# A hybrid decoder block on one core: another order of scores, products and transposes within a slot

## The chip, the core and the metric

One Trainium2 chip, of which the kernel uses one core. The metric is device microseconds of one execution of the whole program; the median of several executions is compared.

## The reference

One layer of a decoder block for 512 positions and width 1024, in fp32. A combined projection gives q, k and v of 16 heads of width 64: eight with dilated sliding-window attention, eight with block-sparse attention. At this length both are causal softmax attention with a bias per head:

```python
u = rmsnorm(h, g_mix[l])
qa, ka, va, qb, kb, vb = jnp.split(u @ w_in[l], 6, axis=-1)
ya = dilated_attention(...)
yb = moba_attention(...)
y = jnp.concatenate([rmsnorm(merge(ya, DIL_WIDTH), g_out_dil[l]),
                     rmsnorm(merge(yb, MOBA_WIDTH), g_out_moba[l])], axis=-1)
h = h + y @ w_out[l]
h = h + memory_cross_attention(rmsnorm(h, g_cross[l]), rmsnorm(mem, g_mem[l]), ...)
h = h + conv_ffn(rmsnorm(h, g_ffn[l]), ...)
```

The output is the RMSNorm of h.

## The kernel before

Every large product is made of three fp32r matmuls with high and low parts (hi by hi, hi by lo, lo by hi). Weights come by DMA on SyncE's queue into three `stage` buffers; ScalarE makes the high part (`hi`, L88), VectorE or GpSimd the low part (`lo`, L97). In the slots GpSimd makes it.

The self-attention runs in 18 **slots** (L800 on), one head further in each. Slot s holds the scores **S** of head s (`s_steps`), the transposes **T** of head s-1 (`t_steps`) and the products with V, **O**, of head s-2 (`o_steps`). Each is a generator: S yields three times (the 512-wide row block, the 384-wide one, and the 128- and 256-wide ones together), T three times (`pt0`, `pt1`, `pt2`), O four times (one 512-wide step from `pt0`, one 384-wide from `pt1`, two 256-wide from `pt2`). The string ORDER has ten positions and says whose turn it is at each. Ahead of each position `fill` puts in other TensorE work up to a due number from the table PACE: steps of the q and k projections of later heads (three 512-wide matmuls a step, L268 to L270), of V's second half (L565 to L567), and of the memory's keys and values. A projection may be blocked until enough heads have their scores, and then positions follow each other with no filler between.

What follows a TensorE step goes through `Later`, a list of stages that are issued a given number of steps later; `L.need` issues them at once if a reader comes first. The chains of this case:

- S: VectorE adds the bias strip and takes the maximum (L701), ScalarE the exponential (L706), VectorE the reciprocal (L711); the normalisation (L713) is VectorE's for the two wide row blocks and GpSimd's for the two narrow ones. The result is `P`, of which there are two buffers.
- T: ScalarE copies the high part out of PSUM (`pt0h` and so on, L251), one step later; VectorE subtracts for the low part (`pt0l`, L256), three steps after that.
- O: ScalarE copies half of the product's bank (`tmp`, L251), then VectorE adds (`y`, L778). For every second head ScalarE makes `Y` and its squares, and GpSimd adds the squares to `ssy` (L283), which the norm matmul L301 reads after the slots.
- q and k: VectorE scales (L259), ScalarE copies, VectorE and GpSimd subtract (L532, L548). For k, two DMAs on SyncE's queue (L535, L536) then copy one half to the other partitions.
- `xm` and `mr` (L466, L256) belong to the memory's preparation, which is spread over the slots.

Each engine works through its own instructions in the order in which they were issued. PSUM has two banks `acc` for projections and a ring of six for all `s`, `t` and `o` tiles, given out in the order in which the steps first come. A slot takes seven of them: three S, three T, one O. The strip of biases for head s+2 is loaded on SyncE's queue when head s begins its scores (`load_strip`, L348).

Of the kernel before, what the change touches and what calls it, by code (L numbers as in the profile page):

```python
# [28 lines left out]
C_MIX, C_OUT, C_CROSS, C_MEM, C_FFN, C_FIN, C_CW, C_CB = 0, 8, 16, 24, 32, 40, 48, 48 + 3 * FT  # L29
NVEC = C_CB + FT  # L30
WARM = 9
ORDER = "OOSOOTSTST"
PACE = ((0, 8), (1, 17), (1.8, 24), (5.0, 64), (5.85, 72), (9.1, 112), (11.8, 136), (18, 209))
RM = 13
XL = {0: (4, 5), 1: (6, 7)}
# [137 lines left out]
def block_kernel(tc, xT, x_tok, memT, mem_tok, w_in, w_out, w_q, w_km, w_vm, w_o, w_gu, w_dn, vecs, relT, onehot,  # L173
                 addend, out):
    nc = tc.nc
    with ExitStack() as ctx:
# [108 lines left out]
        def norm_stages(R, ssq, n, d, exact=False):  # L285


            v = {}

            def s0():  # L290
                v["h"] = tmp(F32R)[:, :n]
                copy(v["h"], ssq)

            def s1():
                v["l"] = tmp(F32R)[:, :n]
                sub(v["l"], ssq, bf(v["h"]))

            def s2():
                v["p"] = ps = bank("t")[:, :n]
                if exact:  # L300
                    nc.tensor.matmul(ps, ones32, ssq, start=True, stop=True)  # L301
                else:
                    nc.tensor.matmul(ps, ones, v["h"], start=True, stop=False)
                    nc.tensor.matmul(ps, ones, v["l"], start=False, stop=True)

            def s3():
                v["r"], v["a"] = tmp()[:, :n], tmp()[:, :n]
                nc.scalar.activation(v["r"], v["p"], AF.Abs_reciprocal_sqrt, scale=1.0 / d, bias=epsb)
                nc.scalar.activation(v["a"], v["r"], AF.Square)

            def s4():
                a = v["a"]
                nc.vector.scalar_tensor_tensor(a, v["p"], d * EPS, a, op0=OP.add, op1=OP.mult)
                nc.vector.tensor_scalar(a, a, -0.5 / d, 1.5, op0=OP.mult, op1=OP.add)
                mul(R, a, v["r"])

            return (s2, s3, s4) if exact else (s0, s1, s2, s3, s4)
# [329 lines left out]
        def fill(x):  # L647

            due = np.interp(x, [a for a, _ in PACE], [b for _, b in PACE])
            while filled[0] < due:  # L650
                r = next(fill_gen, "end")
                if r is BLOCK or r == "end":
                    break
                filled[0] += 1
# [140 lines left out]
        def slot_gens(s):  # L795
            return (o_steps(s - 2) if 0 <= s - 2 < 16 else iter(()),
                    t_steps(s - 1) if 0 <= s - 1 < 16 else iter(()),
                    s_steps(s) if s < 16 else iter(()))

        W.lo_eng = tuple(engs[c] for c in LOE)  # L800
        for s in range(18):
            gens = dict(zip("OTS", slot_gens(s)))
            for i, c in enumerate(ORDER):
                fill(s + i / len(ORDER))
                next(gens[c], None)
            for g in gens.values():
                assert next(g, "end") == "end"
            if s == 16:
                ra_tok = L.chain(*norm_stages(SSQ[0], SSQ[0], S, 512), gap=5)
# [482 lines left out]
```

## Time and profile before

| | us |
|---|---|
| median of 3 executions | 784.73 (784.63 to 784.87) |
| the profiled execution | 784.45 |
| its span on the core | 782.7 |
| TensorE busy | 769.5 |
| VectorE, ScalarE, GpSimd busy | 471.3, 384.3, 180.3 |

The span runs from the first to the last instruction; 1.75 us of the profiled execution lie outside it. A matmul's row in the timeline lasts longer than the distance to the next one, because matmuls overlap; what a matmul costs is read from start to start. The slots lie between about 48 and 247 us of the span.

### The profile page before, as it was taken

What the parts mean: (1) busy time and instruction counts of PE and PEld (TensorE: products, weight loads), DVE (VectorE), ACT (ScalarE), POOL (GpSimd) and SP (SyncE); (2) the same over time, 40 slices, a digit from 0 to 9 for tenths busy, and PEclk for the clock granted to TensorE, in tenths of its full rate; (3) what the DMA queues carried; (4) which work ended last, traced back from release to release, by engine and by line L of the source; (5) the groups of instructions that cost most, each with busy time, mean ns of one, the idle gap of its engine ahead of it and who ended that gap; (6) DMA issues with size and microseconds to landing.
All of it is one profiled execution on the core that took longest, in us unless ns stands there. A gap on an engine that the chain in (4) does not pass through costs nothing.

```text
span 782.7 us, 10336 instructions
## 1 busy us (share of the span) xinstructions
PE 769.5 (98%) x3820; PEld 648.9 (83%) x3820; DVE 471.3 (60%) x874; ACT 384.3 (49%) x753; POOL 180.3 (23%) x179
## 2 busy tenths in 40 slices
PE   9999999999999999999999999999999999999995
PEld 7888989779988888888888888888888888888885
DVE  5656686787663885766486666656666564333324
ACT  5866676677777443544446344343443433322322
POOL 1056566566878550000030000000000000000000
PEclk9999999999999999999999999999999999999998
DMA  9544334334444621211232332232222323333303
GB/s 343 207 141 140 110 123 121 124 92 130 134 155 136 224 99 54 81 55 41 94 108 81 113 103 97 92 108 85 103 94 96 107 78 102 97 96 101 100 21 108
DMA packets 28722, 87.94 MB, mean 112 GB/s; under 512 B 3408, under 2 KB 5584, under 8 KB 28288
## 3 DMA queue, kind: packets, MB, share of 16 engines
q1 hardware_dynamic: 26880, 85.73, 34.0%
q10 hardware_dynamic: 1664, 1.38, 0.5%
q8 instruction: 30, 0.49, 0.3%
q14 instruction: 20, 0.16, 0.1%
q0 software_dynamic: 128, 0.17, 0.1%
HBM read 80.93 MB, written 2.14 MB: 106 GB/s over the span
## 4 chain that ended last, share of the span: by engine, by line
PE 88%; DVE 6%; ACT 4%; DMA 1%; issue 1%; SPq 0%; DVEq 0%; POOL 0%; ACTq 0%; POOLq 0%
PE acc L268 17%; PE acc L270 17%; PE acc L269 17%; PE s L270 6%; PE s L269 6%; PE s L268 6%; PE s L431 2%; PE o L757 2%; PE t L728 1%; DVE P L713 1%; ACT P L706 1%; DVE P L701 1%; PE s L696 1%; PE s L695 1%; DMA mr<-in_memT_dram 1%
## 5 line engine op out<-in xcount | busy, mean ns | idle before, releaser
L88 ACT ACTIVATE hi<-stage 128x512 fp32r<-128x512 f32 (+1 forms) x264 | 152.0, 617 | 182.0 <-PE acc L269 130.2
L97 DVE TENSOR_TENSOR lo<-stage,hi 128x512 fp32r<-128x512 f32 (+1 forms) x178 | 120.2, 711 | 63.0 <-ACT hi L88 63.0
L268 PE MATMUL acc<-X,hi 128*128 128x512 f32 x352 | 140.3, 399 | 0.0
L270 PE MATMUL acc<-X,lo 128*128 128x512 f32 x352 | 137.4, 390 | 0.0
L97 POOL TENSOR_TENSOR lo<-stage,hi 128x512 fp32r<-128x512 f32 x86 | 112.5, 1331 | 29.6 <-ACT hi L88 28.5
L269 PE MATMUL acc<-X,hi 128*128 128x512 f32 x304 | 118.6, 390 | 0.0
L270 PEld LDWEIGHTS acc<-X,lo 128*128 128x128 f32 x352 | 66.0, 188 | 14.2
L268 PEld LDWEIGHTS acc<-X,hi 128*128 128x128 f32 x352 | 66.2, 188 | 11.4 <-issue 0.2
L268 PE MATMUL s<-X,hi 128*128 128x512 f32 x192 | 75.1, 391 | 0.0
L270 PE MATMUL s<-X,lo 128*128 128x512 f32 x192 | 74.7, 389 | 0.0
L268 PE MATMUL acc<-G,hi 128*128 128x512 f32 (+1 forms) x198 | 72.9, 368 | 0.0
L270 PE MATMUL acc<-G,lo 128*128 128x512 f32 (+1 forms) x198 | 72.3, 365 | 0.0
L269 PE MATMUL acc<-G,hi 128*128 128x512 f32 (+1 forms) x198 | 72.3, 365 | 0.0
L269 PE MATMUL s<-X,hi 128*128 128x512 f32 x176 | 68.5, 389 | 0.0
L269 PEld LDWEIGHTS acc<-X,hi 128*128 128x128 f32 x304 | 57.2, 188 | 9.8 <-issue 0.2
L706 ACT ACTIVATE P<-P,st 128x512 f32<-128x512 f32 (+1 forms) x64 | 35.7, 558 | 39.0 <-DVE st L701 38.9
L1084 POOL MEMSET a<- 128x2 f32 x22 | 2.1, 99 | 214.7 <-DVE c L1094 214.0
L1094 DVE SCALAR_TENSOR_TENSOR c<-a,vec,c 128x512 f32<-128x512 f32 x44 | 33.1, 752 | 24.5 <-ACT c L1089 23.8
L268 PEld LDWEIGHTS acc<-G,hi 128*128 128x128 f32 x198 | 37.3, 188 | 6.2
L269 PEld LDWEIGHTS acc<-G,hi 128*128 128x128 f32 x198 | 37.3, 188 | 6.1
L270 PEld LDWEIGHTS s<-X,lo 128*128 128x128 f32 x192 | 36.1, 188 | 7.5
L268 PEld LDWEIGHTS s<-X,hi 128*128 128x128 f32 x192 | 36.0, 188 | 7.6 <-issue 0.2
(264 smaller groups left out, 1536.1 us busy)
## 6 DMA issues: line engine op xcount, KB each, us to landing
stage<-in_w_gu_dram SPq DMA_DIRECT2D x44, 512.0 KB, 3.3
stage<-in_w_in_dram SPq DMA_DIRECT2D x23, 512.0 KB, 3.4
stage<-in_w_dn_dram SPq DMA_DIRECT2D x16, 512.0 KB, 3.5
strip<-scr SPq DMA_DIRECT2D x16, 256.0 KB, 3.9
stage<-in_w_km_dram SPq DMA_DIRECT2D x8, 512.0 KB, 3.5
stage<-in_w_vm_dram SPq DMA_DIRECT2D x8, 512.0 KB, 3.5
stage<-in_w_out_dram SPq DMA_DIRECT2D x8, 512.0 KB, 3.5
stage<-in_w_q_dram SPq DMA_DIRECT2D x8, 512.0 KB, 3.3
```

Source lines behind the costliest of these rows:

```text
L88: self.nc.scalar.activation(self.hi[i][:, a:b], self.stage[i][:, a:b], AF.Copy)
L97: self.lo_eng[part].tensor_sub(self.lo[i][:, a:b], self.stage[i][:, a:b], bf(self.hi[i][:, a:b]))
L268: nc.tensor.matmul(ps, wh[:, w0:w0 + P], xh, start=first, stop=False)
L269: nc.tensor.matmul(ps, wh[:, w0:w0 + P], xl, start=False, stop=False)
L270: nc.tensor.matmul(ps, wl[:, w0:w0 + P], xh, start=False, stop=last)
L431: nc.tensor.matmul(vps[u], (Xl if z == 1 else Xh)[k][:, u * P:(u + 1) * P], w[z // 2][:, ws], start=(k == 0 and z == 0), stop=(k == KT - 1 ...
L695: nc.tensor.matmul(ps[:, o:o + nn], lq, k[:, 0, :nn], start=True, stop=False)
L696: nc.tensor.matmul(ps[:, o:o + nn], lq, k[:, 1, :nn], start=False, stop=True)
L701: nc.vector.tensor_tensor_reduce(v, src, sb[:, :n][:, ::-1], -0.125, 3e38, OP.add, OP.min, accum_out=st[:, i:i + 1])
L706: nc.scalar.activation(v, v, AF.Exp, scale=-1.0, bias=st[:, i:i + 1], accum_out=st[:, 4 + i:5 + i])
L757: nc.tensor.matmul(ps[:, 512 - (b - a):512], V[g][kb][:, j * P:(j + 1) * P], pts[e][pg][z][:, a:b], start=(kb == 0 and z == 0), stop=(kb = ...
L1094: nc.vector.scalar_tensor_tensor(v["c"], v["a"][:, 6 + o:6 + o + S], col(C_CW + o * FT + f), v["c"], op0=OP.mult, op1=OP.add)
```

## The change

ORDER becomes a pair of strings. Slot 0, which has scores alone, keeps the old one. From slot 1 on, scores stand at positions 0, 2 and 8 instead of 2, 6 and 8, products at 1, 3, 4 and 6 instead of 0, 1, 3 and 4, and transposes stay at 5, 7 and 9. The divisor of the position is 10 as before, so the fillers' due numbers are the same.

```diff
-ORDER = "OOSOOTSTST"
+
+ORDER = ("OOSOOTSTST", "SOSOOTOTST")
...
-            for i, c in enumerate(ORDER):
-                fill(s + i / len(ORDER))
+            for i, c in enumerate(ORDER[min(s, 1)]):
+                fill(s + i / 10)
                 next(gens[c], None)
```

Line numbers in the changed file are higher by one below ORDER.

TensorE's order where slot 9 ends and slot 10 begins, before (`t` are transposes, `o` products, `s` scores, `acc` a projection used as filler):

```order
L728 MATMUL t_1772<-ident,P_1562 128x128 x3
L757 MATMUL o_1780<-pt0h_432,V_724 128x512
L757 MATMUL o_1780<-pt0l_433,V_724 128x512
L268 MATMUL acc_1784<-X_110,hi_1592 128x512
L269 MATMUL acc_1784<-X_110,hi_1592 128x512
L270 MATMUL acc_1784<-X_110,lo_1623 128x512
L757 MATMUL o_1780<-pt1h_434,V_724 128x384
L757 MATMUL o_1780<-pt1l_435,V_724 128x384
```

and after:

```order
L729 MATMUL t_1767<-ident,P_1542 128x128 x3
L696 MATMUL s_1782<-K_1685,Q_1592 128x512
L697 MATMUL s_1782<-K_1685,Q_1592 128x512
L269 MATMUL acc_1787<-X_110,hi_1594 128x512
L270 MATMUL acc_1787<-X_110,hi_1594 128x512
L271 MATMUL acc_1787<-X_110,lo_1625 128x512
L758 MATMUL o_1796<-pt0h_432,V_726 128x512
L758 MATMUL o_1796<-pt0l_433,V_726 128x512
L269 MATMUL acc_1787<-X_111,hi_1594 128x512
L270 MATMUL acc_1787<-X_111,hi_1594 128x512
L271 MATMUL acc_1787<-X_111,lo_1625 128x512
L696 MATMUL s_1812<-K_1685,Q_1592 128x384
```

The first score (which reads K5) now stands directly behind the slot's last transpose. The product with `pt0` has five matmuls more between it and that transpose. Behind the rows shown come the second 384-wide score matmul and three more projections, and then the product with `pt1`.

VectorE's order in slot 9, from the first score's normalisation on, before (`ISA` rows are the bias-and-maximum and its read-out):

```order
L713 TENSOR_SCALAR P_1687<-P_1687,st_1688 128x512
L256 TENSOR_TENSOR xm<-mr_1580,xm 128x2x256
L778 TENSOR_TENSOR y_1587<-o_1666,tmp_1714 64x512
L701 ISA P_1687,st_1688<-s_1735,strip_1409 128x384
L701 ISA st_1688 128x1
L256 TENSOR_TENSOR pt0l_433<-t_1723,pt0h_432 128x512
L711 RECIPROCAL st_1688<-st_1688 128x1
L713 TENSOR_SCALAR P_1687<-P_1687,st_1688 128x384
```

and after, from the second score's maximum on:

```order
L702 ISA P_1668,st_1669<-s_1694,strip_1389 128x384
L702 ISA st_1669 128x1
L533 TENSOR_TENSOR K_1685<-tmp_1692,K_1685 64x512
L712 RECIPROCAL st_1669<-st_1669 128x1
L714 TENSOR_SCALAR P_1668<-P_1668,st_1669 128x384
L257 TENSOR_TENSOR xm<-mr_1585,xm 128x2x256
L257 TENSOR_TENSOR pt0l_433<-t_1725,pt0h_432 128x512
L779 TENSOR_TENSOR y_1617<-o_1680,tmp_1739 64x512
L702 ISA P_1668,st_1669<-s_1754,strip_1389 128x128
```

The `y` add moved behind the second score's maximum (`s_1694`) and normalisation and behind `pt0l`; the third score's maximum (`s_1754`) comes behind `y`. The first score's maximum and normalisation stand ahead of these rows in both.

GpSimd's order at the end of the slots, before:

```order
L97 TENSOR_TENSOR lo_2760<-stage_2667,hi_2743 128x512 x2
L283 TENSOR_TENSOR ssy_1965<-ssy_1965,tmp_2773 128x512
L97 TENSOR_TENSOR lo_2789<-stage_2704,hi_2778 128x512 x2
L97 TENSOR_TENSOR lo_2838<-stage_2738,hi_2826 128x512 x2
L97 TENSOR_TENSOR lo_2883<-stage_2767,hi_2868 128x512 x2
```

and after:

```order
L98 TENSOR_TENSOR lo_2756<-stage_2662,hi_2741 128x512 x2
L98 TENSOR_TENSOR lo_2784<-stage_2704,hi_2767 128x512 x2
L284 TENSOR_TENSOR ssy_1999<-ssy_1999,tmp_2787 128x512
L98 TENSOR_TENSOR lo_2838<-stage_2736,hi_2826 128x512 x2
L98 TENSOR_TENSOR lo_2883<-stage_2762,hi_2868 128x512 x2
```

The sum of squares that L301 (L302 after) reads has one more pair of weight operations ahead of it.

## Rows read from the trace of the kernel before

**Rows 1.** The page, part 1: engine, busy us, share, instructions.

```profile
PE 769.5 (98%) x3820; PEld 648.9 (83%) x3820; DVE 471.3 (60%) x874; ACT 384.3 (49%) x753; POOL 180.3 (23%) x179
```

**Rows 2.** TensorE's waits: for whom, us in total, times, longest us.

```profile
PE o L757 <- DVE pt1l L256: 1.1, 4, 0.4
...
PE o L757 <- DVE pt0l L256: 0.5, 1, 0.5
PE o L757 <- ACT pt1h L251: 0.5, 1, 0.5
```

**Rows 3.** TensorE's timeline: start us, us, line, out<-in, [idle before <- releaser].

```profile
64.61 0.33 PE L757 MATMUL o<-pt1h,V 128*128 128x384 f32 x1
64.78 0.34 PE L757 MATMUL o<-pt1l,V 128*128 128x384 f32 x1
...
151.66 0.34 PE L757 MATMUL o<-pt1h,Y 128*128 128x384 f32 x1
152.22 0.44 PE L757 MATMUL o<-pt1l,Y 128*128 128x384 f32 x1 [0.21 <-DVE pt1l L256]
...
153.42 0.39 PE L696 MATMUL s<-K,Q 128*128 128x512 f32 x1
...
155.38 0.28 PE L757 MATMUL o<-pt2l,Y 128*128 128x256 f32 x1
...
160.59 0.49 PE L728 MATMUL t<-ident,P 128*128 128x128 f32 x3
160.83 0.47 PE L757 MATMUL o<-pt0h,V 128*128 128x512 f32 x1
161.76 0.50 PE L757 MATMUL o<-pt0l,V 128*128 128x512 f32 x1 [0.46 <-DVE pt0l L256]
...
162.33 0.39 PE L269 MATMUL acc<-X,hi 128*128 128x512 f32 x1
162.56 0.40 PE L270 MATMUL acc<-X,lo 128*128 128x512 f32 x1
163.41 0.45 PE L757 MATMUL o<-pt1h,V 128*128 128x384 f32 x1 [0.45 <-ACT pt1h L251]
164.24 0.44 PE L757 MATMUL o<-pt1l,V 128*128 128x384 f32 x1 [0.38 <-DVE pt1l L256]
```

**Rows 4.** VectorE's timeline in slot 9 and at the start of slot 10.

```profile
153.94 0.69 DVE L701 CUSTOM_DVE_ANT_0 P<-s,strip 128x512 f32<-128x512 f32 x1 [0.27 <-issue]
...
156.91 0.17 DVE L711 RECIPROCAL st<-st 128x1 f32<-128x1 f32 x1 [1.68 <-ACT P L706]
...
158.01 1.77 DVE L256 TENSOR_TENSOR xm<-mr,xm 128x512 fp32r<-128x512 f32 x1
159.81 0.70 DVE L778 TENSOR_TENSOR y<-o,tmp 64x512 f32<-64x512 f32 x1
160.54 0.56 DVE L701 CUSTOM_DVE_ANT_0 P<-s,strip 128x384 f32<-128x384 f32 x1
...
161.02 0.69 DVE L256 TENSOR_TENSOR pt0l<-t,pt0h 128x512 fp32r<-128x512 f32 x1
...
162.08 0.42 DVE L713 TENSOR_SCALAR P<-P,st 128x384 f32<-128x384 f32 x1
...
163.63 0.55 DVE L256 TENSOR_TENSOR pt1l<-t,pt1h 128x384 fp32r<-128x384 f32 x1
```

**Rows 5.** SyncE's queue in slot 9, and the DMA issues: count, KB, us to landing.

```profile
151.82 0.42 SPq L352 DMA_DIRECT2D strip<-scr  x1
...
156.46 0.47 SPq L536 DMA_DIRECT2D K<-K  x1
```

```profile
K<-K SPq DMA_DIRECT2D x14, 256.0 KB, 3.0
```

**Rows 6.** Timeline of TensorE and GpSimd at the end of the slots.

```profile
246.74 0.28 PE L757 MATMUL o<-pt2l,V 128*128 128x256 f32 x1
...
249.73 1.34 POOL L283 TENSOR_TENSOR ssy<-ssy,tmp 128x512 f32<-128x512 f32 x1 [0.64 <-ACT tmp L278]
251.03 2.54 POOL L97 TENSOR_TENSOR lo<-stage,hi 128x512 fp32r<-128x512 f32 x2
...
254.80 1.02 PE L301 MATMUL t<-ssy,ones 128*128 128x512 f32 x2
```

**Rows 7.** Line 713 (normalisation) on VectorE: duration ns min/median/max, first and last start.

```profile
L713 DVE TENSOR_SCALAR P<-P,st x32: 419/686/1482, 51.3 to 229.2; 128x512 f32<-128x512 f32 x16, 128x384 f32<-128x384 f32 x16
```

## The prediction

> **What bounds the kernel now.** Read first the busy shares, then TensorE's waits, then the timelines of the places they name. TensorE is busy for 769.5 of 782.7 us [rows 1], so only removed gaps or removed work can help, and the change removes no instruction. The waits say where the 18 slots leave TensorE idle: for the second halves of products (O), which need the transposed probabilities `pt1l`, `pt0l` and `pt1h` from VectorE and ScalarE. Together they are 1.1 + 0.5 + 0.5 = 2.1 us of bare idleness [rows 2].
>
> The timeline gives the full price, since a wait also breaks the overlap of neighbouring matmuls. Undisturbed, `pt1l` starts 0.17 us after `pt1h`, and a 512-wide matmul 0.23 us after the one ahead. In slot 9 the step from `pt1h` to `pt1l` is 0.56, so 0.39 is lost; of the four `pt1l` waits in rows 2 two earlier ones are of this kind and are counted at the same price. At the start of slot 10, 160.83 to 161.76 loses 0.93 - 0.23 = 0.70, 162.56 to 163.41 loses 0.85 - 0.23 = 0.62, and 163.41 to 164.24 loses 0.83 - 0.17 = 0.66 [rows 3]. Sum: 3 x 0.39 + 0.70 + 0.62 + 0.66 = **3.15 us**. That is all that the changed positions can win directly.
>
> Why does VectorE come late? In slot 9 it is not behind when the slot's wide score arrives: the bias-and-maximum (L701) starts at 153.94, 0.52 us after the second score matmul at 153.42 and just after an idle stretch. By the end of the slot it is behind. It sat idle for 1.68 us until ScalarE, with other work queued, had done the exponential; then came a 1.77 us `xm` subtraction and the `y` add. Only then did it reach `pt0l` at 161.02 and `pt1l` at 163.63, which TensorE needed at once [rows 3, 4]. So the limit is the way from a score at position 2 to a product at positions 0 and 1 of the next slot, and not VectorE's throughput.
>
> **The change part by part.** *Products later.* A transpose keeps its position, and its reader moves from 0, 1, 3, 4 to 1, 3, 4, 6. In the printed order of slot 10, `pt0` now stands behind two wide score matmuls and three projections, 5 x 0.23 = 1.15 us more than before; that covers the 0.70. For `pt1` the matmuls ahead grow from five to fifteen, two of them 384 wide (0.17 each): 13 x 0.23 + 2 x 0.17 = 3.33 against 1.15, so 2.2 us more. The old lateness there, summed over the three gaps, is 1.98. The lone `pt1` waits of 0.39 gain two positions each. I take all six as gone: **-3.15 us**. The bounds are -2.1 (bare idleness alone) and -3.15.
>
> *Scores earlier.* The first two of a head's three scores reach VectorE two and four positions sooner. The third keeps its position, and its normalised rows are wanted by the next slot's first transpose, seven positions later, as before. I book nothing; if that cover went, the transposes would be next to wait.
>
> *The PSUM ring.* Seven tiles per slot pass through six banks. Before, the product's bank was taken over by the slot's last transpose; now the next slot's first score takes it. From slot 9's last product at position 6 to that score there lie nine projections, two groups of three transposes (0.24 each, by 160.59 to 160.83), four 256-wide matmuls and the product's own end, about 9 x 0.23 + 0.5 + 0.5 + 0.1 = 3.2 us. The bank is free once the `y` add is done. That took from 155.38 to 160.51, 5.1 us, in this slot [rows 3, 4], and the printed VectorE order now puts the second score's maximum and normalisation and `pt0l` ahead of `y`; in rows 4 these take from 160.51 to 162.50, 2.0 us. Against that stand the 1.68 us of idleness, which should shrink, because the first score comes two positions sooner. If it goes wholly, `y` ends at 160.51 + 2.0 - 1.68 = 160.83; if half of it goes, at 161.67. TensorE wants the bank at 160.83 less the 0.39 saved, 160.44. So it waits 0.4 to 1.2 us.
>
> *K5.* The same score is the first reader of K5, whose second copy was issued at 156.46 and takes 3.0 us [rows 5], so it landed at about 159.5. VectorE now serves the first score's maximum (0.69) and normalisation ahead of K5's scaling. With the median normalisation, 0.69, K5 lands at 160.9, with the longest, 1.48, at 161.6 [rows 4, 7]: 0.4 to 1.2 us late. This overlaps the wait for `y` and is not added to it. I book **+0.8 us** for both, the middle; ends 0 and +1.2, with a gain excluded because this place had no wait to remove.
>
> *SyncE's queue.* The loads of the bias strips are issued with the first score, so some now pass a weight load. One such load takes 0.42 us of the queue [rows 5]. Weights are fetched ahead of use, so I book nothing; with that cover gone it would be 0.4 us at a time.
>
> *The end of the slots.* The last product moves two positions towards the norm matmul (L301) that needs its squares. Before, the product at 246.74 was followed by the squares' sum, which ended at 249.73 + 1.34 = 251.07, and L301 came at 254.80 [rows 6]. Now only 24 filler matmuls of 0.23 lie between, 5.5 us, against the 4.3 us that the way took. GpSimd's order now has one more pair of weight operations (2.54 us) ahead of the sum, partly done before the squares arrive. I book nothing; the bound is 4.3 + 2.5 - 5.5 = +1.3.
>
> **Sum.** -3.15 + 0.8 = -2.35 us. The profiled execution took 784.45 us (1.75 outside its span), 0.28 below the median of 784.73. So 782.1 for such an execution, and **782.4** against the median. After the slots TensorE sets the pace again, so the gain should survive.
>
> **A rule weighed.** Operations on VectorE that stay in SBUF vary much: the normalisation L713 takes from 419 to 1482 ns [rows 7], and the `xm` above 1.77 us [rows 4]. The Trainium skill (SBUF — State Buffer, "Who interferes with whom") says that VectorE and GpSimd share a port pair, held for a whole instruction by whichever issued first, while the other is fully blocked. The spread here agrees with that. By that rule, if the second score's normalisation, moved against GpSimd's weight operations, were caught at slot 10, the sum would be 1.06 us worse, -1.3 instead of -2.35.
>
> **The rivals.** (1) *The waits move to the first scores.* If the second score's normalisation grows from 0.42 to 1.48 us [rows 4, 7] on the new way to `y`, slot 10 waits 0.8 + 1.06 = 1.9, and a neighbouring slot perhaps half that surplus, 0.5: -3.15 + 2.4 = -0.75, **784.0**. For it: `y` was 5.1 us behind its product. Against it: the work starts sooner. (2) *The end of the slots waits.* The +1.3 bound comes true: **783.7**. Against it: GpSimd still has idle time there, 0.64 us ahead of the sum [rows 6]. (3) *Slower.* VectorE is as late as before, and `y` comes after what used to follow it, that is from 160.51 to 162.50 in rows 4, 2.0 us. Then slot 10's score waits 5.1 + 2.0 - 3.2 = 3.9 us, and a neighbour half of that, 1.9: -3.15 + 5.8 = +2.65, **787.4**. It decides once the first scores wait over 3.15 us in total. Against it: the second score's work is asked for four positions sooner, so it need not stand in front of `y`. (4) *The change doesn't separate them*: the evacuations could be issued just ahead of the products again. The printed order has them further apart; **784.7**.
>
> **How the numbers follow.** Forecast 0.68 (own range 781.3 to 783.1), rival 1 0.19, rival 2 0.05, rival 3 0.05, rival 4 0.03. A difference under 0.2%, 1.57 us, can't be told from none. Faster than 783.16 holds the forecast and a little of rival 1: 0.70. Slower than 786.3 is rival 3: 0.05. The rest, 0.25, is the same. Low end: all gone with nothing added, 781.6, less half a microsecond for weight and V waits that may go too: 781.1. High end: rivals 1, 2 and 4, 784.7.
>
> **What would show it.** Right: no TensorE wait on `pt0l`, `pt1h` or `pt1l` in the slots; the slot's first score behind at most a short gap, at slot 10; L301 unhindered. Rivals 1 and 3 would show as waits of the first score (L696 in the changed file) on `y` or on K's copy, rival 2 as a gap at L301 (L302 there). I am wrong if the product waits stay.

## The result, and the profile after

The changed kernel took 789.27 us (median of 4, 788.74 to 789.71) against 784.68 before on the same chip: a ratio of 1.0056, 95% interval 1.0042 to 1.0069. It is slower by 4.6 us, where 782.4 was forecast, and lies outside the range of 781.1 to 784.7. (Ratios are worked out from the single executions and need not be the quotient of two medians.) Its profiled execution took 789.71 us with a span of 787.9.

The page of the changed kernel, part 1:

```profile
PE 769.9 (98%) x3820; PEld 648.9 (82%) x3820; DVE 471.9 (60%) x874; ACT 385.1 (49%) x753; POOL 183.4 (23%) x179
```

TensorE works 0.4 us more than in [rows 1], so nearly all of the 5.2 us by which the span grew is idle time of TensorE. Its waits in the changed kernel (for whom, us in total, times, longest us):

```profile
PE acc L568 <- POOL lo L98: 2.3, 3, 1.3
PE acc L269 <- DVE X L257: 1.4, 1, 1.4
...
PE o L758 <- DVE pt2l L257: 1.0, 2, 0.7
PE acc L566 <- DVE V L264: 1.0, 1, 1.0
...
PE o L758 <- DVE pt0l L257: 0.9, 1, 0.9
PE acc L269 <- DVE tmp L260: 0.5, 1, 0.5
...
PE o L758 <- DVE pt1l L257: 0.2, 1, 0.2
```

Two things stand here. The product waits did not go: 1.0 + 0.9 + 0.2 = 2.1 us, as much as in [rows 2], only that `pt2l` now leads. And the fillers wait (`acc`), which the prediction had only as half a microsecond that may go: 2.3 + 1.4 + 1.0 + 0.5 = 5.2 us. L568 wants the low half of a weight from GpSimd; L566 and L269 want an accumulator bank that VectorE has still to empty. The same view of the kernel before has 0.5 us of this:

```profile
PE acc L567 <- POOL lo L97: 0.3, 1, 0.3
PE acc L565 <- DVE V L263: 0.2, 1, 0.2
```

Where in the slots it was lost is read from the timelines: the start of a slot's last score matmul (position 8 in both orders), changed against before, and by how much that difference grows from slot to slot. Slot 2 loses 0.9 us, slots 6 and 7 together 2.0, slots 8 to 10 together 0.5, slot 13 2.2; all others change by less than 0.2. After slot 13 nothing more is lost.

Slot 6 of the changed kernel, on ScalarE, GpSimd and TensorE (timeline: start us, us, engine, line, out<-in, idle before and releaser):

```profile
114.94 0.71 ACT L254 ACTIVATE Y<-y,vec 128x512 fp32r<-128x512 f32 x1
115.56 0.62 ACT L279 ACTIVATE tmp<-y 128x512 f32<-128x512 f32 x1
116.08 0.62 ACT L89 ACTIVATE hi<-stage 128x512 fp32r<-128x512 f32 x1
116.60 1.27 ACT L252 ACTIVATE Q<-tmp 64x512 fp32r<-64x512 f32 x2
...
118.01 1.29 POOL L550 TENSOR_TENSOR Q<-tmp,Q 64x512 fp32r<-64x512 f32 x1 [2.06 <-issue]
119.38 1.62 POOL L284 TENSOR_TENSOR ssy<-ssy,tmp 128x512 f32<-128x512 f32 x1
120.96 2.69 POOL L98 TENSOR_TENSOR lo<-stage,hi 128x512 fp32r<-128x512 f32 x2
...
122.46 0.39 PE L568 MATMUL acc<-lo,X 128*128 128x256 f32 x1 [1.30 <-POOL lo L98]
```

And GpSimd there in the kernel before:

```profile
113.29 1.80 POOL L283 TENSOR_TENSOR ssy<-ssy,tmp 128x512 f32<-128x512 f32 x1 [3.10 <-ACT tmp L278]
...
117.19 1.29 POOL L549 TENSOR_TENSOR Q<-tmp,Q 64x512 fp32r<-64x512 f32 x1 [0.62 <-POOL P L713]
118.56 2.73 POOL L97 TENSOR_TENSOR lo<-stage,hi 128x512 fp32r<-128x512 f32 x2
```

The sum of squares (`ssy`), the end of the chain that an odd head's last product starts, stood in a stretch where GpSimd was otherwise idle. Now the `Y` copy and the squares stand on ScalarE ahead of Q's copies; GpSimd is idle for 2.06 us and starts just behind them (the row names no releaser, but the copies end at 116.60 + 1.27 = 117.87); and the sum comes directly ahead of the weight's low half, which starts at 120.96 instead of 118.56 while its high half had been ready since 116.7. Of these 2.4 us the sum is 1.6; the rest is mostly what the kernel was behind before this slot, 0.7.

Slot 13, VectorE and the matmul that waits, in the changed kernel:

```profile
190.26 0.69 DVE L549 TENSOR_TENSOR Q<-tmp,Q 64x512 fp32r<-64x512 f32 x1 [1.86 <-ACT Q L252]
...
191.59 1.26 DVE L264 SCALAR_TENSOR_TENSOR Y<-y,vec,Y 128x512 fp32r<-128x512 f32 x1
...
195.53 0.16 DVE L712 RECIPROCAL st<-st 128x1 f32<-128x1 f32 x1 [0.78 <-ACT P L707]
195.73 0.42 DVE L714 TENSOR_SCALAR P<-P,st 128x384 f32<-128x384 f32 x1
196.06 0.69 DVE L260 TENSOR_TENSOR tmp<-acc,rx 128x512 f32<-128x512 f32 x1
...
201.91 0.17 DVE L712 RECIPROCAL st<-st 128x2 f32<-128x2 f32 x1 [0.87 <-ACT P L707]
202.18 0.42 DVE L257 TENSOR_TENSOR X<-acc,X 128x256 fp32r<-128x256 f32 x1
...
196.90 0.36 PE L269 MATMUL acc<-xm,hi 128*128 128x256 f32 x1 [0.46 <-DVE tmp L260]
...
202.66 0.39 PE L269 MATMUL acc<-xm,hi 128*128 128x256 f32 x1 [1.41 <-DVE X L257]
```

The operation that frees K7's accumulator bank (L260) runs at 196.06. Ahead of it stand VectorE's wait for Q's copies, Y's low part and two normalisations with a wait for an exponential in between. TensorE waits for it at 196.90. The units of the memory's keys need a bank every 2.9 us (24 matmuls of 0.12) and what stands between. The bank wanted at 202.66 is the other one: its unit's last matmul started at 195.69, and VectorE empties it (`X`, L257) only at 202.18, behind L260, other work and one more wait for an exponential, 0.87 us.

### The profile page after: what moved, and what is told of

It reads as the page before. It is cut to its first block, busy times and chain, and to the rows that moved or that the text cites. A ratio compares the mean times of both kernels' runs of the same rounds, so it can differ in the third digit from the quotient of the medians.

```text
span 787.9 us, 10336 instructions
## 1 busy us (share of the span) xinstructions
PE 769.9 (98%) x3820; PEld 648.9 (82%) x3820; DVE 471.9 (60%) x874; ACT 385.1 (49%) x753; POOL 183.4 (23%) x179
## 4 chain that ended last, share of the span: by engine, by line
PE 87%; DVE 6%; ACT 5%; issue 1%; DMA 0%; DVEq 0%; POOL 0%; SPq 0%; ACTq 0%; POOLq 0%
PE acc L269 17%; PE acc L270 17%; PE acc L271 17%; PE s L270 6%; PE s L269 6%; PE s L271 6%; PE s L432 2%; PE o L758 2%; PE t L729 1%; ACT P L707 1%; DVE P L714 1%; ACT hi L89 1%; DVE tmp L260 1%; DVE P L702 1%; PE s L697 1%
## 5 line engine op out<-in xcount | busy, mean ns | idle before, releaser
L269 PE MATMUL acc<-X,hi 128*128 128x512 f32 x352 | 140.4, 399 | 0.0
L98 POOL TENSOR_TENSOR lo<-stage,hi 128x512 fp32r<-128x512 f32 x86 | 114.7, 1356 | 30.9 <-ACT hi L89 30.0
L269 PEld LDWEIGHTS acc<-X,hi 128*128 128x128 f32 x352 | 66.2, 188 | 11.4 <-issue 0.2
L269 PE MATMUL s<-X,hi 128*128 128x512 f32 x192 | 75.1, 391 | 0.0
L269 PE MATMUL acc<-G,hi 128*128 128x512 f32 (+1 forms) x198 | 72.9, 368 | 0.0
L269 PEld LDWEIGHTS s<-X,hi 128*128 128x128 f32 x192 | 36.1, 188 | 7.7 <-issue 0.2
L269 PEld LDWEIGHTS acc<-G,hi 128*128 128x128 f32 x198 | 37.3, 188 | 6.1
L271 PEld LDWEIGHTS acc<-G,lo 128*128 128x128 f32 x198 | 37.3, 188 | 6.1
```

Of the source, the lines that this page charges most:

```text
L98: self.lo_eng[part].tensor_sub(self.lo[i][:, a:b], self.stage[i][:, a:b], bf(self.hi[i][:, a:b]))
L269: nc.tensor.matmul(ps, wh[:, w0:w0 + P], xh, start=first, stop=False)
L271: nc.tensor.matmul(ps, wl[:, w0:w0 + P], xh, start=False, stop=last)
```

## The experiments

In the diffs an entry of the second list is a letter and its position (the loop calls `fill(s + position / 10)` and then the step). The scores theory: the scores' evacuations, asked for earlier, stand in ScalarE's and VectorE's queues ahead of what the fillers wait for. The products theory: it is the products' later evacuations. For each kernel, from its one profiled execution (the medians below are of more), this is what the slots lose against before, in us, by the starts of the last score matmul:

| kernel | slot 2 | 6, 7 | 8 to 10 | 13 | slots 1 to 15 |
|---|---|---|---|---|---|
| the change | 0.9 | 2.0 | 0.5 | 2.2 | 5.3 |
| scores alone | 1.5 | -1.0 | -1.3 | 0.5 | -0.4 |
| products alone | 0.2 | 1.9 | -0.7 | 6.6 | 7.5 |
| second score back | 0.1 | 1.2 | 0.2 | 2.1 | 3.6 |
| squares sooner | 0.9 | 1.5 | 0.5 | 1.6 | 4.2 |
| last product back | 3.0 | -1.0 | -1.1 | 0.6 | 0.9 |
| last product alone | 0.3 | 1.6 | 1.2 | 2.1 | 5.3 |
| scores from slot 3 | 0.0 | -1.0 | -1.3 | 0.4 | -1.9 |
| evacuation late | 0.3 | 2.1 | 0.8 | 1.4 | 6.9 |
| its first half late | 0.2 | 0.3 | 1.3 | -0.2 | 3.0 |
| its second half late | 0.0 | 1.5 | 1.2 | 1.3 | 4.3 |
| both from slot 3 | 0.0 | -1.0 | -1.1 | 0.7 | -2.0 |

**Which part of the change.** Scores alone (against the changed kernel; of the later diffs of ORDER only the new line is shown):

```diff
-ORDER = ("OOSOOTSTST", "SOSOOTOTST")
+ORDER = (..., "S0 O0 O1 S2 O3 O4 T5 T7 S8 T9".split())
```

> Only the scores move (positions 0, 2 and 8); the products keep 0, 1, 3 and 4. The changed kernel took 789.3 us against 784.7 before; its profile shows 6.4 us of TensorE waits of the filler matmuls (slots 2, 6, 7, 13) against 1.8 before, and product waits unchanged at 3.0. Scores theory (the scores' evacuations, asked for earlier, stand on ScalarE and VectorE ahead of what the fillers wait for): the filler waits stay and so do the product waits, 788 to 790 us, with the gaps in slots 2 and 13 of about 0.9 and 2.2 us. Products theory (the later last product brings its y and squares chain, and GpSimd's sum of squares, ahead of the weights' low halves): the gaps are gone, 784 to 785.5 us.

785.47 us, ratio to before 1.0001 (0.9992 to 1.0010): no difference. (The expectation counts the waits otherwise; as idle time they are the 5.2 and 2.1 us above.) Products alone:

```diff
+ORDER = (..., "O1 S2 O3 O4 T5 S6 O6 T7 S8 T9".split())
```

> Only the products move (positions 1, 3, 4 and 6); the scores keep 2, 6 and 8. Scores theory: no new filler waits; the product waits shrink, since their operands have more time: 781.5 to 784 us. Products theory: the filler waits of the changed kernel are there, slot 6 with 1.4 us first of all: 787 to 789 us.

791.92 us, 1.0092 (1.0078 to 1.0106): slower than the whole change, and 3 us above the range of the products theory; slot 13, and not slot 6, has the longest wait (last section). The scores theory falls. But the table says that scores alone is not nothing either: it loses 1.5 us in slot 2 and gains 2.3 in slots 6 to 10. Its waits:

```profile
PE acc L568 <- POOL lo L98: 1.1, 2, 0.8
...
PE o L758 <- DVE y L779: 0.7, 1, 0.7
...
PE o L758 <- DVE pt0l L257: 0.2, 1, 0.2
```

The waits on `pt1l`, `pt0l` and `pt1h` of [rows 2] fall from 2.1 to 0.2 us although no product has changed its position. The first two do stand further from the transposes, though, by the first score's two matmuls, 2 x 0.23 = 0.46 us. In slot 6 that wasn't needed: VectorE ended `pt1l` at 114.32, and it was used at 116.00. In slot 9 it was: 151.96 and 152.30, 0.34 apart. Slot 2 of this kernel, ScalarE and GpSimd:

```profile
69.72 0.62 ACT L707 ACTIVATE P<-P,st 128x384 f32<-128x384 f32 x1 [1.94 <-DVE st L702]
...
70.95 1.14 ACT L89 ACTIVATE hi<-stage 128x512 fp32r<-128x512 f32 x2
...
71.65 2.51 POOL L98 TENSOR_TENSOR lo<-stage,hi 128x512 fp32r<-128x512 f32 x2 [1.28 <-ACT hi L89]
```

and ScalarE in the kernel before:

```profile
68.89 0.59 ACT L251 ACTIVATE tmp<-o 64x512 f32<-64x512 f32 x1 [0.94 <-PE o L757]
69.39 1.14 ACT L88 ACTIVATE hi<-stage 128x512 fp32r<-128x512 f32 x2
```

The second score's exponential now stands ahead of the weight's high half and waits 1.94 us for VectorE; the weight waits with it, from 69.39 to 70.95. Two more kernels change one thing in the changed order. The second score back at 6:

```diff
+ORDER = (..., "S0 O1 O3 O4 T5 S6 O6 T7 S8 T9".split())
```

> The changed order, but with the second score back at position 6 (the first stays at 0). If it is the second score's exponential and normalisation that hold back VectorE's and ScalarE's queues (four positions earlier, the larger move), the gaps in slots 2 and 13 go: 783 to 786 us. If the first score does it, 788 to 789.5 us. Products theory: 788 to 789.5 us too, with slot 6's gap.

788.07 us, 1.0041 (1.0027 to 1.0055). The total is what the products theory said (a guilty first score was given the same, but scores alone has it at 0 too and costs nothing). Slot 2's loss is gone (0.1), so there the second score is to blame; slot 13 keeps its 2.1. The squares' chain four steps sooner:

```diff
-                tok["y", p] = L.chain(c2, c3, d=3 if p == 7 else 7, gap=1 if p == 7 else 3)
+                tok["y", p] = L.chain(c2, c3, d=3, gap=1 if p == 7 else 3)
```

> The changed order, but the chain after an odd head's last product (Y copy, squares, Y's low part, sum of squares on GpSimd) is issued four steps sooner, which puts it where it stood before the change. Scores theory: slot 6's gap of 1.4 us may go, the rest stays: 787.5 to 789 us. Products theory: nearly all the loss goes: 784 to 785.5 us.

788.58 us, 1.0049 (1.0036 to 1.0061). Slot 6's loss falls from 1.2 to 0.2, which supports the reading of its rows above, but slot 7 takes 0.5 of it back (0.8 to 1.3). By the total the products theory was wrong in this form: it had nearly all of the loss in this chain. The squares are only a part.

**Which product, and its matmuls or its evacuation.** What is common to the bad kernels is the last product at 6. The last product back at 4 in the changed order:

```diff
+ORDER = (..., "S0 O1 S2 O3 O4 O4 T5 T7 S8 T9".split())
```

> The changed order, but with the last product (the step whose end frees the product's bank and starts its evacuation) back at position 4, behind the third; the others stay at 1, 3 and 4, the scores at 0, 2 and 8. So far: scores alone 785.5 us, products alone 791.9, changed kernel 789.3, before 784.6. Last-product theory (the evacuation of a finished product, tmp copy, y add and after an odd head the squares, comes two positions later on ScalarE, VectorE and GpSimd, and what the fillers wait for comes behind it): the gaps in slots 6, 7 and 13 go, slot 2's of 0.9 to 1.5 us stays, 783 to 785.5 us. First-products theory (the three earlier steps do it): 788 to 790 us.

784.34 us (782.52 to 785.49), 0.9993 (0.9984 to 1.0002). Against the changed kernel slots 6 and 7 lose 3.0 us less, slots 8 to 10 1.6 and slot 13 1.6; slot 2's loss stays. The 3.0 in the table is one execution, in which the clock fell behind that wait (last section). The last product alone at 6 in the order of before:

```diff
+ORDER = (..., "O0 O1 S2 O3 T5 S6 O6 T7 S8 T9".split())
```

> The order of before, with the last product alone moved from 4 to 6. Last-product theory: the gaps of the products-alone kernel (1.1 in slot 6, 0.7 in slot 7, 6.6 in slot 13 with the low clock that followed), so 788 to 792 us. First-products theory: no change, 784 to 785.5 us.

789.97 us, 1.0073 (1.0061 to 1.0086): this one step, moved by two positions, costs as much as the change. The places are only in part those expected: slot 13 loses 2.1 and not 6.6, and most of the idle time is product waits. Its first waits:

```profile
PE o L758 <- DVE pt1l L257: 4.3, 5, 1.3
PE acc L568 <- POOL lo L98: 2.0, 2, 1.4
```

The scores alone again, with slots 0 to 2 in the old order (against scores alone):

```diff
-            for c, i in ORDER[min(s, 1)]:
+            for c, i in ORDER[s > 2]:
```

> Scores alone, but with slots 0 to 2 in the order of before. In the scores-alone kernel slot 2 lost 1.5 us against before (low halves of v2's weights late), and slots 6 to 10 gained 2.3. If slot 2's loss is due to the scores of that slot: 782.5 to 784.2 us. If the lateness only moves on to slot 3 or later: 784.5 to 786 us.

782.33 us, 0.9974 (0.9964 to 0.9985), a little better than expected. Slot 2's loss is gone and did not move on. This kernel is faster than before and than scores alone.

The last of these leaves TensorE's order as it was before and only issues the evacuation of a finished product later:

```diff
-            L.chain(c0, c1, d=GO[0], gap=GO[1])
+            L.chain(c0, c1, d=GO[0] + 4, gap=GO[1])
...
-                tok["y", p] = L.chain(c2, c3, d=3 if p == 7 else 7, gap=1 if p == 7 else 3)
+                tok["y", p] = L.chain(c2, c3, d=7 if p == 7 else 11, gap=1 if p == 7 else 3)
```

> The order of before on TensorE, unchanged; only the evacuation of each finished product (tmp copy, y add, and after odd heads Y copy, squares and their sum) is issued four steps later, about where the changed kernel issues it. If the place of this evacuation in the other engines' queues is what costs: 787 to 792 us, with filler gaps in slots 6, 7 and 13. If it is the place of the products among TensorE's matmuls: 784 to 785.5 us.

791.33 us, 1.0091 (1.0077 to 1.0104). Its waits, and GpSimd and TensorE in its slot 6:

```profile
PE o L757 <- DVE pt1l L256: 2.6, 5, 1.1
PE acc L567 <- POOL lo L97: 2.6, 2, 1.9
PE o L757 <- DVE pt0l L256: 1.3, 3, 0.6
```

```profile
119.61 1.84 POOL L549 TENSOR_TENSOR Q<-tmp,Q 64x512 fp32r<-64x512 f32 x1 [2.06 <-issue]
121.53 1.28 POOL L283 TENSOR_TENSOR ssy<-ssy,tmp 128x512 f32<-128x512 f32 x1
122.78 1.45 POOL L97 TENSOR_TENSOR lo<-stage,hi 128x512 fp32r<-128x512 f32 x1
...
124.27 0.39 PE L567 MATMUL acc<-lo,X 128*128 128x256 f32 x1 [1.85 <-POOL lo L97]
```

It is slot 6 of the changed kernel over again: the same 2.06 us of GpSimd's waiting, the sum, the low half, and TensorE behind it. Not one matmul has moved in TensorE's order, so a late place of the evacuation in the other engines' queues is shown to cost as much by itself as the change did. It is not the same loss in every place: slot 7, where 0.8 us was expected, loses nothing here, and product waits in slots 4, 5 and 9 are new.

**Its two halves, and two candidates.** The first half late:

```diff
-            L.chain(c0, c1, d=GO[0], gap=GO[1])
+            L.chain(c0, c1, d=GO[0] + 4 * (p < 7), gap=GO[1])
```

> The order of before on TensorE; only the first half of a product's evacuation (ScalarE's tmp copy and VectorE's y add) is issued four steps later, for all head pairs but the last. Both halves late took 791.3 us against 784.5. Split by halves: if the tmp copy and y add carry the loss, 788 to 791 us, with the gap at the middle matrix's accumulators (slot 13); if the squares carry it, 784 to 786 us.

787.49 us, 1.0038 (1.0025 to 1.0050). The size was nearly foreseen (0.5 us under the range), the place was not: slot 13 loses nothing, and the loss is product waits, 4.6 us on `pt1l` in five places against 1.1 in [rows 2]. The second half late:

```diff
-                tok["y", p] = L.chain(c2, c3, d=3 if p == 7 else 7, gap=1 if p == 7 else 3)
+                tok["y", p] = L.chain(c2, c3, d=7 if p == 7 else 11, gap=1 if p == 7 else 3)
```

> The order of before on TensorE; only the second half (after odd heads: Y copy and square on ScalarE, Y's low part on VectorE, sum of squares on GpSimd) is issued four steps later. If the squares carry the loss: 787 to 791 us, with slot 6's gap, where TensorE waits for the low half of a weight behind the sum on GpSimd. If the tmp copy and y add carry it: 784 to 786 us.

788.38 us, 1.0044 (1.0031 to 1.0058), with slot 6's gap as expected (1.9 us in slot 6). Both halves carry the loss: 3.0 and 4.3 us in the table, 6.9 together. The first candidate is the kernel with the last product back, from slot 3 on:

```diff
+ORDER = (..., "S0 O1 S2 O3 O4 O4 T5 T7 S8 T9".split())
...
+            for c, i in ORDER[s > 2]:
```

> Scores at 0, 2 and 8, first three products at 1, 3 and 4, the last product at 4 too, and all of it from slot 3 on; slots 0 to 2 in the order of before. The same from slot 1 on took 784.3 us and lost 3.0 in slot 2. If that loss belongs to slot 2 alone, and the first products' later positions cost nothing: 781 to 782.5 us, no slower than scores alone from slot 3 (782.3). If the first products' places cost something too: 782.5 to 784.

781.91 us, 0.9966 (0.9955 to 0.9978): the fastest of all. Against scores alone from slot 3 the intervals overlap, so beside the scores' move the first three products' later places are worth nothing that can be measured.

The second is scores alone from slot 3 on, less two slots:

```diff
+            for c, i in ORDER[s > 2 and s not in (11, 13)]:
```

> Scores alone from slot 3 on (782.3 us), but slots 11 and 13 in the order of before, since these two lost 0.4 us each there. If those losses belong to these slots: 781.3 to 782.0 us. If the old order there brings product waits back in slots 12 and 14: 782.0 to 783.0 us.

783.27 us, 0.9985 (0.9976 to 0.9994): a miss, no better than leaving these slots alone. Slot 13 lost 0.7 with the old order too, so its 0.4 was not the doing of that slot's scores. Slot 11 lost 0.9 instead of 0.4, and its rows show a product wait there, 0.64 us for `pt0l` at 171.63, which is what the expectation's second case had, though for slots 12 and 14.

## Why the prediction was wrong

- **The step that failed** is *Products later*. It counted the reader's side alone: more matmuls between a transpose and the product that reads it. The last product also starts a chain on three engines, and the step "the last product moves two positions" was costed only for the end of the slots. Four steps of delay of that chain, with nothing else changed, cost 6.9 us in the slots. So "I take all six as gone: -3.15 us" held the operands' times fixed while the change made them later: late evacuation alone brings 2.6 + 1.3 = 3.9 us of waits on `pt1l` and `pt0l`, against 1.6 in [rows 2]. In the changed kernel slot 10 shows it, on VectorE and TensorE:

```profile
162.33 0.16 DVE L712 RECIPROCAL st<-st 128x1 f32<-128x1 f32 x1 [1.74 <-ACT P L707]
162.53 1.00 DVE L714 TENSOR_SCALAR P<-P,st 128x384 f32<-128x384 f32 x1
163.45 1.77 DVE L257 TENSOR_TENSOR xm<-mr,xm 128x512 fp32r<-128x512 f32 x1
165.14 0.68 DVE L257 TENSOR_TENSOR pt0l<-t,pt0h 128x512 fp32r<-128x512 f32 x1
...
163.12 0.49 PE L729 MATMUL t<-ident,P 128*128 128x128 f32 x3
163.61 0.47 PE L696 MATMUL s<-K,Q 128*128 128x512 f32 x1
...
165.88 0.50 PE L758 MATMUL o<-pt0h,V 128*128 128x512 f32 x1 [0.87 <-DVE pt0l L257]
```

`pt0l` ends at 165.82, 2.7 us after the start of the last transposes, against 161.71 - 160.59 = 1.1 before [rows 3, 4]: 1.6 us later, where the product had gained 1.15. Here it is the second score's normalisation and `xm` that stand ahead of `pt0l`.
- **Scores earlier**, booked at nothing, was two terms. The gain that the prediction wanted comes from here: 2.3 us in slots 6 to 10. In slot 6 VectorE is ready sooner, much as the prediction's paragraph on VectorE's lateness said; in slot 9 the 0.46 us that the first score puts ahead of the products was needed as well. How much each gives was not tried. The loss is slot 2: 0.9 us in the changed kernel, 1.5 with the scores alone.
- **"Weights are fetched ahead of use, so I book nothing"** looked at the DMA only. After the fetch a weight has two operations more, on ScalarE and GpSimd, and these stand in the same queues as all evacuations. That is where the waits grew from 0.3 to 2.3 us.
- **The ring and K5, +0.8,** came to 0.25 at most: in the rows above the first score starts 0.49 us after the transposes, where 0.24 is undisturbed. By the times the first copy of K5, the one that this head reads (issued at 160.65, 3.0 us on the way), is the likely cause, and not the second, which was issued at 161.96. The ring step had the wrong tiles. The six banks are not given out in strict turn: in the program before, the product's bank goes to the next slot's product, in the changed one to the next slot's second score, and the product itself gets the bank of its own first transposes, which `pt0l` has to empty. So the matmul at 165.88 waits for `pt0l` though it reads `pt0h`. In scores alone the bank goes to the next product, and there, not at a score, the wait for `y` stands, near the size that was booked:

```profile
161.74 0.47 PE L758 MATMUL o<-pt0h,V 128*128 128x512 f32 x1 [0.69 <-DVE y L779]
```
- **The end of the slots, 0,** was right: L302 starts at 260.03 against 254.80 for L301 [rows 6], 5.23 us later, which is the loss of the slots and no more.
- **The rivals.** Rival 3 had the sign, with the wrong place: its price of +2.65 hung on first scores waiting for `y`. None had the fillers as the ones that wait; the 0.5 us of it in the kernel before stood in the prediction's low end as time to be won.
- **The rule weighed** was priced at slot 10, and there the second score's normalisation did take 1.00 us instead of 0.42 while GpSimd worked on a low half; that made `pt0l` later, not the first score. Over the slots the normalisation took 420 to 1560 ns (419 to 1482 before [rows 7]). By the rows' times, in both kernels every one of 0.5 us or more overlapped a GpSimd operation, and those that overlapped none took 0.42 or 0.49.
- That the engines take their work in the order of issue stands in the account of the kernel before; the Trainium skill (TensorE: Matmul & The Clock Gate, "Architectural detail: the array is 16× 32×32, not 1× 128×128") says the same of ScalarE's and VectorE's queues, strictly first in, first out. The rows of slot 2 agree: the high half waits behind an exponential that itself waits 1.94 us.

What is read from rows and not tried alone: that in slot 2 it is the exponential on ScalarE, and not VectorE, that holds the weight back, and what stands in whose way in slots 7, 10 and 13. Shown is that in slot 2 the second score's place does it, and that the last product's place, by its evacuation alone if need be, costs what the change lost.

## What to carry to other kernels

A step moved in TensorE's order moves its evacuation on every engine behind it: list those operations with the new neighbours in each queue, and ask what late work now stands behind them, weight splits and accumulator banks first. A kernel that is 98% busy on one engine has little to win and much to lose, so the waits that are near zero before (0.3 us on a low half here) are the ones to price. And try the kinds of step apart, and slot by slot: here the scores' part gained in slots 6 to 10 and lost in slot 2, the first products' part did nothing that could be measured, the loss went when the last product went back, and the change without that step and from slot 3 on is 0.34% faster than before.

## What was not expected of the hardware

In products alone, slot 13 lost 6.6 us though its gap is 3.6. The timeline and the stretches around it (windows: us, busy of PE, PEld, DVE, ACT, POOL, granted clock, DMA share, GB/s):

```profile
202.68 0.58 PE L269 MATMUL acc<-xm,hi 128*128 128x256 f32 x1 [3.60 <-DVE X L257]
```

```profile
202.60:208.60 6.00, 5.92 (x24) 5.73 (x25) 2.44 (x7) 2.07 (x5) 6.00 (x6) 0.50 0.40 124
208.60:215.00 6.40, 6.40 (x55) 6.40 (x55) 3.39 (x10) 4.50 (x10) 2.81 (x3) 1.00 0.59 196
```

After 3.6 us without work TensorE was granted 0.50 of its clock, the 1.2 GHz level, for the next 6 us, and then 2.4 again: a wait cost nearly twice its length. With the last product back, three gaps of 0.48, 0.84 and 0.27 us within slot 2 were followed by 0.62 in the stretch from 73 to 76 us; in scores alone, with gaps of 0.46, 0.84 and 0.27 in the same place, the clock stayed at 1.00 (first line the last product back, second line scores alone):

```profile
73.00:76.00 3.00, 2.73 (x15) 2.52 (x14) 1.88 (x2) 1.17 (x3) 2.34 (x2) 0.62 0.44 106
64.00:80.00 16.00, 14.43 (x95) 12.89 (x94) 10.51 (x25) 10.50 (x23) 11.41 (x11) 1.00 0.43 118
```

The kernel doesn't decide it alone: of the 11 executions of scores alone six took 785.5 to 785.8 us with a mean granted clock of 0.994, and five, the profiled one among them, 784.1 to 784.2 with 0.996. So short gaps may or may not cost this, and the 3.0 us of that one execution is not the gaps' own price.
